# PSUM tiles as single banks, two VectorE instructions for the gating layer's normalised v, and another issue order, in a two-layer diffusion backbone

## The chip, the cores and the metric

The kernel runs on one core of a Trainium2 chip. The metric is the device time of one execution in microseconds (us); where several runs are shown it is their median. The core's engines are TensorE (PE in the profile; PEld is its weight loading), VectorE (DVE), ScalarE (ACT), GpSimd (POOL) and SyncE (SP), which here only issues DMAs.

## The reference

512 latent tokens of width 1024 pass through two layers, with 256 context tokens beside them in the first. Each layer is a token mixer and a SwiGLU feed-forward network (FFN); each of the four sub-layers has an RMS norm before and after it and takes shift, scale and gate rows from the conditioning (adaLN). The first mixer is windowed grouped-query attention, the second a gated MLP whose v half is normalised over its width and mixed over the 128 tokens of a chunk:

```
def layernorm(x, g, b):
    mu = jnp.mean(xf, axis=-1, keepdims=True)
    var = jnp.mean(jnp.square(xf - mu), axis=-1, keepdims=True)
    y = (xf - mu) * lax.rsqrt(var + LN_EPS)
    return (y * g + b)

def chunk_gmlp(h, w_in, b_in, ln_g, ln_b, w_s, b_s, w_o):
    z = jax.nn.gelu(h @ w_in + b_in, approximate=False)
    u, v = jnp.split(z, 2, axis=-1)
    v = layernorm(v, ln_g, ln_b).reshape(bsz, n // CHUNK, CHUNK, B_GROUPS, B_GROUP_W)
    mixed = jnp.einsum('gpq,bnqgc->bnpgc', w_s, v) + b_s.T[None, None, :, :, None]
    return (u * mixed.reshape(bsz, n, B_WIDTH)) @ w_o
```

The FFN is `(silu(h @ w_a) * (h @ w_b)) @ w_out` with a hidden width of 2816. All of it is in float32.

## The kernel before

Every product of matrices is computed as three matmuls in fp32r: each operand is split into a high part, which ACT writes (`w_hi`, `v_hi`, the high half of `H`), and a low part, the rest, which DVE mostly writes (`w_lo`, `v_lo`). hi x hi, hi x lo and lo x hi are added up in PSUM. The 512 tokens lie in four tiles `t` of 128. The stages, by the start of the span: the first norms, keys and queries, attention (to about 240 us), attention's output projection (`WO0`, to 300), FFN0's input half (to 500) and output half (to 625), the gating layer's v and u (to 705), its mixes and its output (`GO`, to 795), FFN1 (to the end).

PSUM has eight banks of 512 float32 for each partition. Outside attention the kernel takes its PSUM tiles from `slot`, which gives tiles of 1024, two banks, of which four exist. Most uses need one bank: `u_part` and `y` write the two halves apart, `mixed`, `head` and `ada_ps` use one half and leave the other. From FFN1's products on, `one_banked` changes to a pool of eight tiles of one bank each.

The FFN's input half forms each block of hidden columns from seven products of quarters, after Strassen (`product`, tile `f`, L1416). A block `n` has three chains in PSUM: 0 takes products 1, 6, 7 and 4, chain 1 takes 5 and 3, chain 2 takes 2. `keep` (ACT, tile `fc`, L1423) copies a chain out between two products. Before the change, in FFN0, chains 0 and 1 of a block lie in one tile, one bank each (`chain`). The output half works the same way on its first columns (`product7`, L1599, tiles `y`, with the adds of L1616 on the results), and plainly on the rest (`plain7`, L1630; its steps are `work_9_t` and `work_10_t` for two units of weights and tile `t`).

At the end of each sub-layer a tile `t` runs through a `Chain`: `square_y` (ACT) and `gain_y` (DVE, L1116) read y from PSUM, then come the power for `ry` on POOL, `add_x` (L1120), `square_x`, the power for `rx`, `gain_x` on POOL (L1132), `shift_x` (L1136), `turn` (PE transposes into `hT`, L1143), and `turned_hi` and `turned_lo`, which write the next `H`. The projection adds an earlier part of y in `merge` (L1104).

In the gating layer tile `t` of v passes a `VChain`: `add` (L1808), `gelu`, `mean`, `var`, `rstd`, `norm` (L1826), `gain` (L1830), `bias` on POOL (L1833), then `v_hi` on ACT and `v_lo` on DVE. The mixes (`mixed`, eight groups of twelve matmuls of 128 columns, L264 to L266) need all four tiles. Beside all this, the rows of adaLN are formed from streamed weights (`add_chunk`, DVE L374, into `acc`; `total`, PE, into `ada_ps`).

The order on each engine is fixed in the program. Steps are entered by `at(time, step)`; a table of names, ORDER, ranks them, and `run_plan` issues them by rank. Each engine executes its own instructions in the order in which they were issued.

Of the kernel before, what the change touches and what calls it, by code (L numbers as in the profile page):

```python
# [157 lines left out]
f0sum_low_S2 f0head_3_2 f0sum_low_S1 f0sum_high_S3 f0part_low_2_1 f0sum_low_S4 f0part_low_2_3 f0sum_low_S3 whigh_43_0  # L158
work_9_0 work_10_0 wlow_43_0 c0square_y#2 whigh_43_1 c0gain_y#2 wfetch_44 work_9_1 c0rstd_y#2 c0add_x#2 work_9_2
# [5 lines left out]
c2shift_x_0#2 c3rstd_y#2 <lambda>_0_0 <lambda>_3_2 <lambda>_0_1 c2shift_x_1#2 c1turned_lo_0#2 c2turn_0#2 c2turn_1#2  # L165
c3add_x#2 whigh_45_1 c1turned_lo_1#2 c3gain_x#2 c2turned_hi_0#2 m2fetch_chunk_0 m2fetch_chunk_1 c3square_x#2
c2turned_hi_1#2 <lambda>_1_0 <lambda>_1_1 c3rstd_x#2 c3shift_x_0#2 c3turn_0#2 c3shift_x_1#2 c2turned_lo_1#2 c3turn_1#2
c2turned_lo_0#2 wlow_45_1 c3turned_hi_1#2 c3turned_hi_0#2 <lambda>_2_0 c3turned_lo_0#2 m2fetch_chunk_2 <lambda>_3_0
<lambda>_2_1 wlow_45_0 <lambda>_3_1 c3turned_lo_1#2 wfetch_46 wfetch_47 m2start#2 lend_u0 v_part_0_(2,) row_in_0
whigh_46_0 row_in_2 whigh_46_1 wlow_46_0 whigh_47_0 row_in_1 wfetch_48 wlow_46_1 m2add_chunk_0 whigh_47_1 bias_in  # L170
v_part_0_(3,) wlow_47_0 m2add_chunk_1 m2fetch_chunk_3 v_part_3_(2,) v_part_1_(2,) v0add m2add_chunk_2 m2fetch_chunk_4
v0gelu m2fetch_chunk_5 v0mean wlow_47_1 ws_in m2add_chunk_3 v0var v0rstd v_part_1_(3,) m2add_chunk_4 m2fetch_chunk_6
v0norm m2add_chunk_5 m2fetch_chunk_7 v_part_2_(2,) v0gain whigh_48_0 whigh_48_1 v1add m2add_chunk_6 u_part_0_0 v1gelu
v0bias v1mean m2add_chunk_7 wlow_48_1 m2fetch_gain#2 v_part_3_(3,) wlow_48_0 m2halve_512#2 m4start#2 m4fetch_chunk_0
m2halve_0#2 v1var v_part_2_(3,) ws_high v1rstd wfetch_49 v0hi v1norm m4fetch_chunk_1 ws_low v1gain v0lo v1bias
m2total_0_slot m2done_0#2 v2add m4add_chunk_0 m4fetch_chunk_2 u_part_0_1 m2total_512_slot m2done_512#2 v2gelu v1hi
v1lo whigh_49_0 u_part_1_0 u_part_1_1 v2mean whigh_49_1 gelu_u_0_0 v3add v2var gelu_u_0_1 wlow_49_0 m4add_chunk_1
m4fetch_chunk_3 wfetch_50 v3gelu v2rstd wlow_49_1 m4fetch_chunk_4 v2norm v3mean v2gain m4add_chunk_2 v3var u_part_2_0
m4add_chunk_3 m4fetch_chunk_5 v2bias v3rstd wfetch_51 m4add_chunk_4 m4fetch_chunk_6 u_part_2_1 v3norm whigh_50_0
v3gain m4add_chunk_5 m4fetch_chunk_7 gelu_u_1_0 gelu_u_1_1 v2hi v2lo m4add_chunk_6 v3bias v3hi v3lo m4add_chunk_7  # L180
m4fetch_gain#2 mixed_0 whigh_50_1 mixed_bias_0 mixed_1 mixed_u_0 mixed_bias_1 wlow_50_0 mixed_5 m4halve_0#2 mixed_3
mixed_u_1 mixed_4 gelu_u_2_0 mixed_2 wlow_50_1 whigh_51_0 mixed_bias_3 mixed_u_3 u_part_3_0 m4halve_512#2 whigh_51_1
mixed_6 mixed_bias_2 mixed_u_2 wlow_51_0 m4total_0_slot mixed_bias_4 mixed_u_4 mixed_bias_5 gelu_u_2_1 wlow_51_1
mixed_u_5 u_part_3_1 m4done_0#2 mixed_7 mixed_bias_6 m4total_512_slot m4done_512#2 gelu_u_3_0 gelu_u_3_1 mixed_u_6
mixed_bias_7 mixed_u_7 whigh_55_0 work_2_0#2 work_3_0#2 whigh_55_1 c0square_y#3 work_2_1#2 wlow_55_1 work_3_1#2
wfetch_56 whigh_56_0 wlow_55_0 whigh_56_1 work_2_2#2 c1square_y#3 c0rstd_y#3 c0gain_y#3 c0add_x#3 m3total_0_slot
m3total_512_slot c0gain_x#3 c0square_x#3 m3done_0#2 work_3_2#2 wlow_56_0 c0rstd_x#3 m3done_512#2 c2square_y#3
c1gain_y#3 c1rstd_y#3 c0shift_x_1#3 c0shift_x_0#3 c1add_x#3 c0turn_0#3 c1gain_x#3 c2gain_y#3 c0turn_1#3 c1square_x#3
c1rstd_x#3 c2rstd_y#3 wfetch_57 c0turned_hi_0#3 work_2_3#2 c1shift_x_0#3 c0turned_hi_1#3 c2add_x#3 c2gain_x#3
work_3_3#2 c1shift_x_1#3 c1turn_0#3 c1turn_1#3 c0turned_lo_0#3 c3square_y#3 c0turned_lo_1#3 c3rstd_y#3 c3gain_y#3  # L190
c2square_x#3 f1head_0_0 c1turned_hi_0#3 c2rstd_x#3 c1turned_hi_1#3 wlow_56_1 f1part_high_2_0 f1first_half_1 c3add_x#3
f1first_half_0 c2shift_x_0#3 f1part_high_2_2 c3square_x#3 c3gain_x#3 c1turned_lo_0#3 f1head_0_1 c3rstd_x#3 f1head_0_2
c2turn_0#3 c1turned_lo_1#3 c2shift_x_1#3 f1diff_2_1 f1first_half_1#2 f1head_1_0 c3shift_x_0#3 f1first_half_0#2
f1diff_2_3 c2turn_1#3 f1head_1_1 c2turned_hi_1#3 c2turned_hi_0#3 c3shift_x_1#3 c3turn_0#3 c3turn_1#3 c3turned_hi_0#3
f1diff_2_2 c3turned_hi_1#3 f1sum_a_S3 f1part_high_2_1 c2turned_lo_0#3 f1sum_a_S2 c2turned_lo_1#3 f1part_low_2_0
f1sum_a_S3#2 f1sum_a_S1 c3turned_lo_0#3 f1head_1_2 f1sum_a_S2#2 f1sum_a_S4 f1sum_a_S1#2 f1head_2_0 f1head_2_1
f1sum_a_S4#2 f1sum_high_S2 f1diff_2_4 c3turned_lo_1#3 f1part_high_2_3 f1head_2_2 f1sum_high_S4 f1part_low_2_1
f1head_3_0 f1sum_low_S4 f1part_low_2_2 f1head_3_1 f1sum_high_S3 wfetch_58 f1sum_high_S1 f1head_3_2 f1sum_low_S1
f1sum_low_S2 f1part_low_2_3 f1sum_low_S3
# [4 lines left out]
def backbone_kernel(ctx: ExitStack, tc: tile.TileContext, a, out):  # L204
# [144 lines left out]
    class Ada:  # L349
# [37 lines left out]
        def total(self, c, bank):  # L387
            st = self.stages.pop(c)
            self.ps[c] = ps = bank("ada_ps")[:, 0:512]
            for z in range(2):  # L390
                nc.tensor.matmul(ps, ones, st[:, z * 512:(z + 1) * 512], start=z == 0, stop=z == 1)
# [688 lines left out]
    def slot(name):  # L1080
        return psM_p.tile([P, D], F32, name=name, tag="b2", bufs=4)
# [9 lines left out]
    class Chain:  # L1091


        def __init__(self, t, ps, G, nxt, part):
            self.t, self.all_ps, self.G, self.nxt, self.ms, self.part = t, ps, G, nxt, [], part

        def y(self, c0, c1):
            if self.part is not None:
                return self.part[:, c0:c1]
            ps = self.all_ps[self.t]  # L1100
            return ps[c0 // 512] if isinstance(ps, tuple) else ps[:, c0:c1]
# [11 lines left out]
        def gain_y(self, c0=0, c1=D):  # L1113
            if c0 == 0:
                self.tmp = big("tmp")
            nc.vector.tensor_tensor(out=self.tmp[:, c0:c1], in0=self.y(c0, c1), in1=self.G[:, c0:c1], op=ALU.mult)  # L1116
# [22 lines left out]
        def turn(self, z):  # L1139
            if z == 0:  # L1140
                self.pt = slot("hT")
            for k in range(4 * z, 4 * z + 4):
                nc.tensor.transpose(self.pt[:, k * P:(k + 1) * P], self.tmp[:, D + k * P:D + (k + 1) * P], ident)  # L1143

        def parts(self, z):
            H, c = self.nxt[2], slice(self.t * P, (self.t + 1) * P)
            return (H[:, 4 * z:4 * z + 4, c], H[:, KC + 4 * z:KC + 4 * z + 4, c],
                    self.pt[:, z * 512:(z + 1) * 512].rearrange("p (k s) -> p k s", k=4))
# [11 lines left out]
    def down(u0, nu, lhs, G_of, nxt_of, head, lend=None, part={}, first=None, also=None, seven=None, bg=None, bg_steps=0):  # L1160
# [4 lines left out]
        ps, sts, left = seven.whole if seven else {}, {}, bg_steps  # L1165
# [7 lines left out]
        def work(v, t):  # L1173
# [5 lines left out]
            if v == v0:  # L1179
                ps[t] = slot(f"y{t}")  # L1180
# [65 lines left out]
    class FFN:  # L1246
        def __init__(self, layer):
            self.layer, self.u0, self.head_ps, self.slot, self.bank = layer, F1[layer], {}, slot, slot
# [26 lines left out]
        def head(self, t, n):  # L1275
# [8 lines left out]
            for k in range(4 * n, 4 * n + 4):  # L1284
                hi, lo = (w[:, (k % 2) * 512:(k % 2 + 1) * 512] for w in parts[(k % 4) // 2])
                mm3(self.head_ps[t][:, 0:512], H[:, k, c], H[:, KC + k, c], hi, lo, k == 0, k == KC - 1)

        def head_gated(self, t):
            pv = self.head_ps[t][:, 0:512].rearrange("p (n z s) -> p n z s", n=2, z=2)
# [8 lines left out]
        def head_turn(self, t, s):  # L1298
            pt = self.slot("fat")
# [12 lines left out]
        def quarters(self):  # L1312
            self.A, self.raw_at, self.T, self.X, self.ps, self.pair, self.c, self.g = {}, {}, {}, {}, {}, {}, {}, {}
# [8 lines left out]
        def first_half(self, q, c):  # L1322

            name = ("S1", "S4")[q]
            if c.t == 0:
                self.sums[name] = self.sum_tile(stage32)
            nc.scalar.copy(out=self.sums[name][:, :, c.t * P:(c.t + 1) * P],
                           in_=c.pt[:, q * 512:(q + 1) * 512].rearrange("p (k s) -> p k s", k=4))
# [4 lines left out]
        def sum_a(self, name, c):  # L1333
# [5 lines left out]
            a21, a22 = (c.pt[:, z * 512:(z + 1) * 512].rearrange("p (k s) -> p k s", k=4) for z in range(2))  # L1339
# [131 lines left out]
        def one_banked(self):  # L1471

            psM.__exit__(None, None, None)
            self.psE = pool("psE", space=PSUM)
            pe = self.psE.__enter__()
            self.bank = self.slot = lambda name: pe.tile([P, 512], F32, name=name, tag="bk", bufs=8)

        def rest(self, nxt_of, head, rows=(), **kw):
# [30 lines left out]
            for i in range(KC * len(sums)):  # L1509
# [8 lines left out]
                if k == KC - 1:  # L1518
                    at(b + .1, e.fetch_gain)
                    for z in range(2):  # L1520
                        at(b + T * (.25 + .85 * z), e.halve, z * 512, nc.vector)
                        at(b + T * (.25 + .85 * z) + 3.7, e.total, z * 512, self.bank)
# [515 lines left out]
```

## Time and profile before

| | |
|---|---|
| three runs | 1132.28, 1132.56, 1134.19 us |
| profiled execution | 1132.03 us, span 1130.3 us |
| mean granted PE clock | 0.991 of full |
| busy | PE 98%, DVE 85%, ACT 54%, POOL 23% |
| read from HBM | 171.71 MB, 154 GB/s over the span |

In the rows of groups, the columns are line, engine, operation, out<-in, shapes, count, then busy time and the mean of one in ns, then the idle time of the engine before them and what ended it. In the rows of a timeline, the first number is the start, the second the duration, and the bracket the idle time before with its releaser. A row of waits gives the total, the count and the longest. A row of windows gives, for each engine, busy time and count of instructions, and near its end the granted clock. Matmuls are pipelined, so a row's duration is longer than the step to the next.

### The profile page before, as it was taken

The numbers are of one execution on the slowest core, as the hardware profiler recorded it, in microseconds if no ns is written. First come the engines' busy times: TensorE is split into PE (matmuls) and PEld (weight loads), VectorE is DVE, ScalarE is ACT, GpSimd is POOL, SyncE is SP. The second block draws the span as 40 slices with busy tenths as digits, with TensorE's granted clock in tenths as the row PEclk, the third lists the DMA queues.
The fourth block names the chain that finished last, engine by engine and source line by source line (L and its number), as shares of the span: only waits on it lengthen the run. The fifth ranks groups of instructions, "written<-read, shape, count | busy, mean of one in ns | idle before, by whom it ended". The sixth has DMA issues, their size and how long they took to land.

```text
span 1130.3 us, 17929 instructions
## 1 busy us (share of the span) xinstructions
PE 1107.2 (98%) x7038; PEld 973.2 (86%) x7038; DVE 959.9 (85%) x1398; ACT 614.0 (54%) x1049; POOL 265.6 (23%) x245
## 2 busy tenths in 40 slices
PE   8999999999999999999999999999999999999997
PEld 5789877768899999998887788888899999998876
DVE  6788988959999999988977879867988888879985
ACT  6357768666544555455564534246555555546552
POOL 2347575514600000002312314005400000002400
PEclk9999999999999999999999999799999999999999
DMA  9742332233255554469935376443134333459921
GB/s 370 283 138 93 114 112 76 76 138 106 93 166 174 183 170 163 153 223 278 218 63 168 109 255 233 138 161 108 41 131 149 132 111 133 150 177 322 176 35 75
DMA packets 47577, 174.97 MB, mean 155 GB/s; under 512 B 4602, under 2 KB 8954, under 8 KB 36356
## 3 DMA queue, kind: packets, MB, share of 16 engines
q1 hardware_dynamic: 40580, 161.24, 40.7%
q0 software_dynamic: 6912, 12.59, 6.6%
q8 instruction: 55, 0.90, 0.3%
q14 instruction: 30, 0.25, 0.1%
HBM read 171.71 MB, written 2.10 MB: 154 GB/s over the span
## 4 chain that ended last, share of the span: by engine, by line
PE 84%; DVE 9%; ACT 3%; issue 3%; DMA 1%; POOL 0%; SPq 0%; DVEq 0%; POOLq 0%; ACTq 0%
PE f L1416 32%; PE y L1599 13%; PE y L272 7%; PE y L1630 5%; PE v L272 4%; PE s_ps L882 3%; PE o_ps L935 2%; PE pT_ps L915 2%; DVE w_lo L220 2%; PE q_ps L264 1%; PE q_ps L266 1%; PE q_ps L265 1%; PE kv L264 1%; DVE a_sum L1342 1%; PE kv L265 1%
## 5 line engine op out<-in xcount | busy, mean ns | idle before, releaser
L1416 PE MATMUL f<-H,w_hi 128*128 128x256 f32 x960 | 178.1, 283 | 0.0
L1587 POOL DMA_DIRECT2D t<-in_w x48 | 42.3, 933 | 492.6 <-PE y L1630 216.1
L1416 PEld LDWEIGHTS f<-H,w_hi 128*128 128x128 f32 x960 | 150.0, 192 | 0.5
L1416 PE MATMUL f<-H,w_lo 128*128 128x256 f32 x480 | 135.7, 283 | 0.0
L1599 PE MATMUL y<-w_hi,s 128*128 128x512 f32 x448 | 120.8, 390 | 0.8 <-DVE y L1616 0.8
L1416 PE MATMUL f<-S,w_hi 128*128 128x256 f32 x640 | 120.0, 285 | 0.0
L217 ACT CAST w_hi<-w_raw 128x1024 fp32r<-128x1024 f32 x90 | 94.3, 1051 | 39.4 <-PE y L1599 12.2
L217 ACT CAST w_hi<-T 128x1024 fp32r<-128x1024 f32 x80 | 83.7, 1048 | 57.0 <-PE f L1416 27.1
L1423 ACT COPY fc<-f 128x256 f32<-128x256 f32 x120 | 44.6, 373 | 119.0 <-PE f L1416 116.8
L220 DVE TENSOR_TENSOR w_lo<-w_raw,w_hi 128x1024 fp32r<-128x1024 f32 (+1 forms) x77 | 92.8, 1208 | 9.0 <-ACT w_hi L217 9.0
L1599 PEld LDWEIGHTS y<-w_hi,s 128*128 128x128 f32 x448 | 83.9, 188 | 19.0 <-DVE y L1616 1.3
L1416 PEld LDWEIGHTS f<-S,w_hi 128*128 128x128 f32 x640 | 99.5, 192 | 0.4
L220 DVE TENSOR_TENSOR w_lo<-T,w_hi 128x1024 fp32r<-128x1024 f32 x80 | 97.2, 1215 | 0.0
L1416 PEld LDWEIGHTS f<-H,w_lo 128*128 128x128 f32 x480 | 92.1, 192 | 0.0
L1416 PE MATMUL f<-S,w_lo 128*128 128x256 f32 x320 | 90.6, 283 | 0.5 <-DVE w_lo L220 0.5
L374 DVE SCALAR_TENSOR_TENSOR acc<-ada_k,sc,acc 128x1024 f32<-128x1024 f32 x56 | 75.4, 1346 | 5.7 <-DMA ada_k<-in_ada 3.6
L1599 PE MATMUL y<-w_lo,s 128*128 128x512 f32 x224 | 69.1, 390 | 0.6 <-DVE w_lo L220 0.6
L909 POOL TENSOR_SCALAR p<-p,st 128x512 f32<-128x512 f32 (+1 forms) x64 | 55.8, 885 | 43.3 <-DVE st L905 25.1
L1416 PE MATMUL f<-H,x 128*128 128x256 f32 x480 | 64.2, 283 | 0.0
L1416 PEld LDWEIGHTS f<-S,w_lo 128*128 128x128 f32 x320 | 61.3, 192 | 0.7 <-DVE w_lo L220 0.7
L888 DVE CUSTOM_DVE_ANT_0 s_ps<-s_ps,mask,nsink 128x512 f32<-128x512 f32 (+1 forms) x64 | 51.8, 816 | 11.7 <-PE s_ps L882 9.5
L272 PE MATMUL y<-w_hi,st 128*128 128x512 f32 x224 | 61.2, 391 | 0.3 <-ACT uT L1858 0.3
(263 smaller groups left out, 2891.0 us busy)
## 6 DMA issues: line engine op xcount, KB each, us to landing
w_raw<-in_w SPq DMA_DIRECT2D x67, 1024.0 KB, 5.1
ada_k<-in_ada SPq DMA_DIRECT2D x56, 512.0 KB, 5.8
ada_raw<-in_ada SPq DMA_DIRECT2D x12, 1024.0 KB, 5.1
w<-in_w SPq DMA_DIRECT2D x12, 1024.0 KB, 8.8
t<-in_w POOLq DMA_DIRECT2D x48, 256.0 KB, 5.9
ada<-in_ada SPq DMA_DIRECT2D x8, 1024.0 KB, 12.2
t<-in_w SPq DMA_DIRECT2D x8, 1024.0 KB
w_raw<-in_w SPq DMA_DIRECT2D x10, 512.0 KB
```

Source lines behind the costliest of these rows:

```text
L217: nc.scalar.copy(out=hi, in_=src)
L220: (eng or nc.vector).tensor_tensor(out=lo, in0=src, in1=hi.bitcast(F32), op=ALU.subtract)
L272: nc.tensor.matmul(dst, l, w[:, n * 512:(n + 1) * 512], start=first and i == 0, stop=last and i == 2)
L374: nc.vector.scalar_tensor_tensor(out=self.acc, in0=self.raws.pop(k), scalar=sc[:, k:k + 1], in1=self.acc, op0=ALU.mult, op1=ALU.add)
L882: nc.tensor.matmul(dst, self.qT[:, j, :], keys, start=i == 0, stop=i == 1)
L888: nc.vector.tensor_tensor_reduce(out=s, in0=s, in1=self.msk, scale=-1.0, scalar=nsink[:, h:h + 1], op0=ALU.add, op1=ALU.min, accum_out=sel ...
L909: nc.gpsimd.tensor_scalar(out=p, in0=p, scalar1=self.st[:, 12 + j:13 + j], scalar2=1.0, op0=ALU.mult, op1=ALU.mult)
L1416: nc.tensor.matmul(dst, l[:, w], r[:, k, :], start=first and k == 0 and j == 0, stop=k == 3 and j == 2, skip_group_check=True)
L1423: nc.scalar.copy(out=self.c[n][:, i * 256:(i + 1) * 256], in_=self.ps[n, 1 if i == 1 else 0])
L1587: nc.gpsimd.dma_start(out=self.tt[:, p * D + 512 * i:p * D + 512 * (i + 1)], in_=a["w"][F2[self.layer] + 1 + 2 * p + i][:, c:c + 512], acc ...
L1599: nc.tensor.matmul(self.bank7(i, j), st[:, c:c + P], w[:, z * 512:(z + 1) * 512], start=i == 1 and p == 0 and l == 0 and z == 0, stop=p == ...
L1630: nc.tensor.matmul(self.y[t][n], st[:, x + t * P:x + (t + 1) * P], parts[h][w][:, n * 512:(n + 1) * 512], start=v == 0 and h == 0 and i == ...
```

## The change

1. `slot` gives one bank, eight of which exist; `slots` gives a pair of such tiles for y and v. Tiles `f`, `u`, `mix`, `hT`, `fat`, `fa` and `ada_ps` become single banks, and chains 0 and 1 of a block are two tiles. `one_banked` goes. An instruction that read 1024 columns of a two-bank tile becomes two of 512: `merge`, `square_y`, `gain_y` and VChain's `add`.
2. VChain's `norm` goes. `gain` forms (w - mu) x gain and `bias` forms that x r + bias, each one scalar_tensor_tensor on DVE; `bias` leaves POOL. `gain` needs no longer the power `rv`, `bias` does.
3. ORDER is another one from FFN0's output half on.

```
-        return psM_p.tile([P, D], F32, name=name, tag="b2", bufs=4)
+        return psM_p.tile([P, 512], F32, name=name, tag="bk", bufs=8)
+
+    def slots(name):
+        return tuple(slot(f"{name}{n}") for n in range(2))
+
+    def halves(c0, c1):
+        return [(c, min(c + 512, c1)) for c in range(c0, c1, 512)]
...
         def merge(self):
-            nc.vector.tensor_tensor(out=self.part, in0=self.all_ps[self.t], in1=self.part, op=ALU.add)
+            for c0, c1 in halves(0, D):
+                p = self.part[:, c0:c1]
+                nc.vector.tensor_tensor(out=p, in0=self.all_ps[self.t][c0 // 512], in1=p, op=ALU.add)
...
         def square_y(self, c0=0, c1=D):
-            self.ms.append(mean_square(self.y(c0, c1), "msy"))
+            for c in [(c0, c1)] if self.part is not None else halves(c0, c1):
+                self.ms.append(mean_square(self.y(*c), "msy"))
...
-            nc.vector.tensor_tensor(out=self.tmp[:, c0:c1], in0=self.y(c0, c1), in1=self.G[:, c0:c1], op=ALU.mult)
+            for a0, a1 in [(c0, c1)] if self.part is not None else halves(c0, c1):
+                nc.vector.tensor_tensor(out=self.tmp[:, a0:a1], in0=self.y(a0, a1), in1=self.G[:, a0:a1], op=ALU.mult)
...
         def chain(self, n, ch):
 
-            if ch == 1 and self.bank is slot:
-                return self.pair[n][:, 512:768]
-            self.pair[n] = ps = self.bank(f"f{ch}")
-            return ps[:, 0:256]
+            return slot(f"f{ch}")[:, 0:256]
...
-        def one_banked(self):
-
-            psM.__exit__(None, None, None)
-            self.psE = pool("psE", space=PSUM)
-            pe = self.psE.__enter__()
-            self.bank = self.slot = lambda name: pe.tile([P, 512], F32, name=name, tag="bk", bufs=8)
...
-            nc.vector.tensor_tensor(out=self.v, in0=v_ps[self.t], in1=rows[0], op=ALU.add)
+            for n, (c0, c1) in enumerate(halves(0, D)):
+                nc.vector.tensor_tensor(out=self.v[:, c0:c1], in0=v_ps[self.t][n], in1=rows[0][:, c0:c1], op=ALU.add)
...
-        def norm(self):
-            nc.vector.tensor_scalar(out=self.v, in0=self.w, scalar1=self.mu[:, 0:1], scalar2=self.r,
-                                    op0=ALU.subtract, op1=ALU.mult)
-
         def gain(self):
-            nc.vector.tensor_tensor(out=self.v, in0=self.v, in1=rows[1], op=ALU.mult)
+            nc.vector.scalar_tensor_tensor(out=self.v, in0=self.w, scalar=self.mu[:, 0:1], in1=rows[1],
+                                           op0=ALU.subtract, op1=ALU.mult)
 
         def bias(self):
-            nc.gpsimd.tensor_tensor(out=self.v, in0=self.v, in1=rows[2], op=ALU.add)
+            nc.vector.scalar_tensor_tensor(out=self.v, in0=self.v, scalar=self.r, in1=rows[2],
+                                           op0=ALU.mult, op1=ALU.add)
...
-f0sum_low_S2 f0head_3_2 f0sum_low_S1 f0sum_high_S3 f0part_low_2_1 f0sum_low_S4 f0part_low_2_3 f0sum_low_S3 whigh_43_0
-work_9_0 work_10_0 wlow_43_0 c0square_y#2 whigh_43_1 c0gain_y#2 wfetch_44 work_9_1 c0rstd_y#2 c0add_x#2 work_9_2
+f0sum_low_S2 f0head_3_2 f0sum_low_S1 f0sum_high_S3 f0part_low_2_1 f0sum_low_S4 f0part_low_2_3 f0sum_low_S3 work_9_1
+whigh_43_0 work_9_0 work_10_0 wlow_43_0 c0square_y#2 whigh_43_1 c0gain_y#2 wfetch_44 c0rstd_y#2 c0add_x#2 work_9_2
```

What the table does on PE near the end of FFN0's output half, where the last of `product7` (L1599) meets `plain7` (L1630 before, L1626 after). The number in a tile's name after `y` is its `t`; after the change a second digit is the bank. Before:

```order
L1599 MATMUL y3_5860<-w_lo_6469,s7_6464 128x512 x2
L1599 MATMUL y3_5860<-w_hi_6468,s7_6464 128x512 x2
L1630 MATMUL y0_5893<-w_lo_6496,st_6510 128x512 x2
L1630 MATMUL y0_5893<-w_hi_6495,st_6510 128x512 x2
L1630 MATMUL y0_5893<-w_hi_6514,st_6529 128x512 x2
L1630 MATMUL y0_5893<-w_lo_6515,st_6529 128x512 x2
L1630 MATMUL y0_5893<-w_hi_6514,st_6529 128x512 x2
L1630 MATMUL y0_5893<-w_hi_6533,st_6536 128x512 x2
L1630 MATMUL y0_5893<-w_lo_6534,st_6536 128x512 x2
L1630 MATMUL y0_5893<-w_hi_6533,st_6536 128x512 x2
```

After, at the same place:

```order
L1599 MATMUL y30_5899<-w_lo_6511,s7_6506 128x512 x2
L1599 MATMUL y30_5899<-w_hi_6510,s7_6506 128x512 x2
L1626 MATMUL y10_5958<-w_lo_6538,st_6552 128x512
L1626 MATMUL y11_5959<-w_lo_6538,st_6552 128x512
L1626 MATMUL y10_5958<-w_hi_6537,st_6552 128x512
L1626 MATMUL y11_5959<-w_hi_6537,st_6552 128x512
L1626 MATMUL y00_5933<-w_hi_6526,st_6529 128x512
L1626 MATMUL y01_5934<-w_hi_6526,st_6529 128x512
L1626 MATMUL y00_5933<-w_lo_6527,st_6529 128x512
L1626 MATMUL y01_5934<-w_lo_6527,st_6529 128x512
```

Tile 1 has taken the place of tile 0 around the last products, and tile 0's unit 9, twelve matmuls, now stands behind them, ahead of its unit 10. From tile 0's last matmul to the first `hT` PE has 60 matmuls before and 48 after.

On DVE, the end of v's chains in the gating layer. Before, from the last `norm` on:

```order
L1826 TENSOR_SCALAR vtmp<-vtmp,mu,rv 128x1024
L1830 TENSOR_TENSOR vtmp<-vtmp,row_6898 128x1024
L374 SCALAR_TENSOR_TENSOR acc<-ada_k,sc,acc 128x1024
L220 TENSOR_TENSOR v_lo<-vtmp,v_hi 128x1024
L374 SCALAR_TENSOR_TENSOR acc<-ada_k,sc,acc 128x1024
L220 TENSOR_TENSOR v_lo<-vtmp,v_hi 128x1024
L374 SCALAR_TENSOR_TENSOR acc<-ada_k,sc,acc 128x1024
```

After, from the last `gain` (L1823) on; L1827 is `bias`:

```order
L1823 SCALAR_TENSOR_TENSOR vtmp<-vtmp,mu,row_6964 128x1024
L374 SCALAR_TENSOR_TENSOR acc<-ada_k,sc,acc 128x1024
L220 TENSOR_TENSOR v_lo<-vtmp,v_hi 128x1024
L374 SCALAR_TENSOR_TENSOR acc<-ada_k,sc,acc 128x1024
L1827 SCALAR_TENSOR_TENSOR vtmp<-vtmp,rv,row_6965 128x1024
L220 TENSOR_TENSOR v_lo<-vtmp,v_hi 128x1024
L374 SCALAR_TENSOR_TENSOR acc<-ada_k,sc,acc 128x1024
```

The bias of the last tile now stands on DVE between the last two `v_lo`, with the high part of that tile, on ACT, still to come after it; POOL's part is gone. On PE the order of the mixes moves as well: before, 72 mixes stand between the first three pairs of u and the next, and 12 after that; now 84 stand in one run.

More of the change, by code (lines that the diff above doesn't have):

```diff
@@ L1139, in turn @@
         def turn(self, z):
[L1140 to L1143, printed above, removed]
+            self.pt[z] = slot("hT")
+            for k in range(4):
+                c = D + z * 512 + k * P
+                nc.tensor.transpose(self.pt[z][:, k * P:(k + 1) * P], self.tmp[:, c:c + P], ident)
         def parts(self, z):
@@ L1892, in backbone_kernel @@
             at(5.45 * t + 2.72 * (u - 2), v_part, t, (u,))
[L1893 to L1894 removed]
+        for b, f in ((0, c.add), (1.2, c.gelu), (2.5, c.mean), (2.8, c.var), (4.1, c.rstd), (3.3, c.gain),
+                     (5, c.bias), (6.4, c.hi), (7.5, c.lo)):
             at(5.45 * (t + 1) + b, f)
```

122 lines of the change are left out of this document (57 added, 65 removed).

## The prediction

> **What bounds the kernel now.** I read the page first, for the busy times, the granted clock and the chain that ended last.
>
> ```profile
> PE 1107.2 (98%) x7038; PEld 973.2 (86%) x7038; DVE 959.9 (85%) x1398; ACT 614.0 (54%) x1049; POOL 265.6 (23%) x245
> PEclk9999999999999999999999999799999999999999
> PE 84%; DVE 9%; ACT 3%; issue 3%; DMA 1%; POOL 0%; SPq 0%; DVEq 0%; POOLq 0%; ACTq 0%
> ```
>
> PE is busy 98% of the span. The change takes no matmul away, so it can gain only what PE loses: the 2% in which it waits, and the slice with the 7, in which PE was busy at a lower clock. VectorE (85%) is second, so work that is given to it is not free wherever PE already waits for it. Next I read the waits of PE, taking those in stages that the change touches.
>
> ```profile
> PE f L1416 <- ACT fc L1423: 1.9, 3, 1.0
> PE mix L266 <- DVE v_lo L220: 1.5, 1, 1.5
> PE y L1630 <- DVE w_lo L220: 1.4, 1, 1.4
> PE hT L1143 <- DVE tmp L1136: 1.3, 2, 0.8
> PE y L1599 <- DVE y L1616: 0.8, 1, 0.8
> PE fa L266 <- DVE H L220: 0.7, 1, 0.7
> PE ada_ps L391 <- ACT row L396: 0.7, 1, 0.7
> ```
>
> Together 8.3 us are within reach, plus what the lower clock costs. Everything below is a change against the profiled execution, 1132.03 us (span 1130.3 and 1.7 around it), which is 0.5 below the median of the runs, 1132.56.
>
> **FFN0's products.** The timeline of ACT and PE at the longest of the three waits for `fc`:
>
> ```profile
> 431.42 1.05 ACT L217 CAST w_hi<-T 128x1024 fp32r<-128x1024 f32 x1 [1.68 <-DVE T L1373]
> 431.75 0.40 PE L1416 MATMUL f<-H,w_hi 128*128 128x256 f32 x2
> 432.00 0.28 PE L1416 MATMUL f<-H,w_lo 128*128 128x256 f32 x1
> 432.89 0.36 ACT L1423 COPY fc<-f 128x256 f32<-128x256 f32 x1
> 433.31 0.51 PE L1416 MATMUL f<-s,w_hi 128*128 128x256 f32 x2 [1.03 <-ACT fc L1423]
> ```
>
> The product that starts at 433.31 writes chain 1. The copy that it waited for reads chain 0, which lies in the other bank of the same tile; ACT reached it late, behind a cast that was itself waiting for `T`. With a tile for each bank this product needs only the copy of its own chain, which stands earlier on ACT. The next product of chain 0, twelve matmuls later, still needs the late copy: twelve at 0.125 us (two from 431.75 to 432.00) are 1.5 us, more than the 1.0 waited. So I take the three waits as gone: 1.9, and 0.5 for the pipeline's restarts, **-2.4**. Bounds: -2.4, and 0 if ACT's lateness simply reaches the next product.
>
> **Split instructions.** What one full-width instruction and two halves cost, and what the change of the gating layer exchanges, by the groups:
>
> ```profile
> L1116 DVE TENSOR_TENSOR tmp<-y,row 128x1024 f32<-128x1024 f32 x10 | 12.2, 1218 | 4.6 <-ACT junk L235 4.6
> L1116 DVE TENSOR_TENSOR tmp<-y,row 128x512 f32<-128x512 f32 x8 | 5.5, 689 | 5.3 <-ACT junk L235 5.2
> L235 ACT ACTIVATE junk<-y 128x1024 bf16<-128x1024 f32 x10 | 10.2, 1024 | 16.0 <-PE y L1630 8.1 <-PE y L272 7.9
> L235 ACT ACTIVATE junk<-y 128x512 bf16<-128x512 f32 x8 | 4.8, 597 | 15.4 <-PE y L1630 15.3
> L235 ACT ACTIVATION_READ_ACCUMULATOR junk<-y 128x1 f32 x18 | 3.5, 195 | 0.0
> L1808 DVE TENSOR_TENSOR vtmp<-v,brow 128x1024 f32<-128x1024 f32 x4 | 4.9, 1216 | 5.0 <-PE v L272 5.0
> L1826 DVE TENSOR_SCALAR vtmp<-vtmp,mu,rv 128x1024 f32<-128x1024 f32 x4 | 3.2, 812 | 2.0 <-POOL rv L245 2.0
> L1120 DVE SCALAR_TENSOR_TENSOR x<-tmp,ry,x 128x1024 f32<-128x1024 f32 x15 | 19.2, 1280 | 3.3 <-POOL ry L245 3.1
> L1830 DVE TENSOR_TENSOR vtmp<-vtmp,row 128x1024 f32<-128x1024 f32 x4 | 4.9, 1220 | 0.0
> L1833 POOL TENSOR_TENSOR vtmp<-vtmp,row 128x1024 f32<-128x1024 f32 x4 | 12.3, 3066 | 11.2 <-DVE vtmp L1830 11.2
> ```
>
> A split gain costs DVE 2 x 0.689 - 1.218 = 0.16 us more, a split square costs ACT 2 x (0.597 + 0.195) - (1.024 + 0.195) = 0.37 more, so a tile's way from y to the next H grows by 0.53. Ten tiles are concerned: the end of attention's projection, of FFN0 and of the gating layer. While PE has matmuls of other tiles to do, this is hidden. Without that cover it costs 0.5 a tile. At the projection's end I charge one tile and its merge, **+0.6** (0 to 2.1).
>
> **FFN0's output half.** The timeline of PE and ACT, with two rows that give the pace of 512-wide matmuls:
>
> ```profile
> 594.05 0.73 PE L1599 MATMUL y<-w_hi,s 128*128 128x512 f32 x2 [0.83 <-DVE y L1616]
> 605.34 0.74 PE L1630 MATMUL y<-w_lo,st 128*128 128x512 f32 x2 [1.44 <-DVE w_lo L220]
> 606.58 1.02 ACT L235 ACTIVATE junk<-y 128x1024 bf16<-128x1024 f32 x1 [1.40 <-PE y L1630]
> 616.84 1.07 PE L1630 MATMUL y<-w_hi,st 128*128 128x512 f32 x4
> 617.75 0.62 PE L1630 MATMUL y<-w_lo,st 128*128 128x512 f32 x2
> 620.02 1.04 PE L1143 MATMUL hT<-ident,tmp 128*128 128x128 f32 x8
> ```
>
> The wait at 594.05 is again for the other bank of a tile, and goes. The one at 605.34 is a weight whose low part is late. `work_9_1`, twelve matmuls of tile 1, now stand ahead of it, which are 12 x 0.2275 = 2.7 us of cover (0.91 us for four), so it goes too: 0.8 + 1.4 and two restarts, 2.6. But tile 0 is complete no earlier, since those twelve now precede it: 606.5 less 2.6 plus 2.7. From its first square to the first `hT` are 13.4 us before (606.58 to 620.02), under 60 matmuls (13.7 us); now 48 stand there, 10.9 us. PE would come 2.5 too early by the old way of tile 0. That way gets shorter, because before its shifts stood behind tile 1's gain and add, and tile 1 is now complete 24 matmuls after tile 0 instead of 36, so they are done by then; it gets longer by 0.5. I take half of the 2.6: **-1.2** (-2.2 to +0.5).
>
> **The gating layer.** The timeline around the last v tile:
>
> ```profile
> 701.60 3.31 POOL L1833 TENSOR_TENSOR vtmp<-vtmp,row 128x1024 f32<-128x1024 f32 x1 [2.25 <-DVE vtmp L1830]
> 702.56 3.42 DVE L220 TENSOR_TENSOR v_lo<-vtmp,v_hi 128x1024 fp32r<-128x1024 f32 x1
> 707.11 1.21 DVE L220 TENSOR_TENSOR v_lo<-vtmp,v_hi 128x1024 fp32r<-128x1024 f32 x1
> 708.38 0.33 PE L266 MATMUL mix<-ws_hi,v_lo 128*128 128x128 f32 x1 [1.50 <-DVE v_lo L220]
> ```
>
> The same DVE instruction takes 3.42 beside POOL's bias and 1.21 alone. Per tile DVE loses norm and gain, 0.81 + 1.22, and gets two scalar_tensor_tensor, which at the 1.28 of the chain's add into x make +0.5, with +0.16 for the split add. It gains some 2 us for each bias that no longer runs beside it, and the chain loses 3.07 of POOL for about 1.3 of DVE. The last v_lo should be over 2 us earlier against PE, the wait was 1.5: **-1.3**, with 0.2 kept for a chunk of weights that lands late (0 to -1.7).
>
> **The gating layer's output.** Eight banks instead of four pairs free the `ada_ps` wait of 0.7. The waits for `hT` and `H` behind it (0.8 and 0.7) may take it back, with 0.5 a tile from the splits: **-0.4** (-1.4 to +2.1).
>
> **The clock.** The windows view, cut at the borders at which the granted clock changes, 3.41 us apart:
>
> ```profile
> 78.63:82.04 3.41, 1.83 (x7) 1.16 (x7) 1.95 (x4) 3.38 (x5) 3.29 (x4) 1.00 0.00 0
> 430.20:433.61 3.41, 2.38 (x20) 2.17 (x19) 2.32 (x4) 2.19 (x4) 0.00 (x0) 1.00 0.47 133
> 706.68:710.10 3.42, 1.92 (x17) 1.78 (x17) 3.42 (x4) 0.80 (x3) 0.95 (x1) 1.00 0.03 6
> 713.51:716.92 3.41, 3.41 (x17) 3.41 (x18) 3.41 (x5) 1.26 (x3) 0.00 (x0) 0.50 0.23 38
> 720.34:723.75 3.41, 3.41 (x9) 2.64 (x9) 3.38 (x4) 0.00 (x0) 0.00 (x0) 0.50 0.54 197
> ```
>
> From 710.10 to 723.75, four such windows, the clock is 0.50. Half of that, 6.8 us, is the most that full clock can return; as 128-wide mixes run a little better than half, I take 6.5. The window ahead of it holds the mix wait: 17 matmuls of 128 columns, 2,176, where a full stream of 512-wide ones passes 15 x 512 = 7,680, a share of 0.28. The window at 78.63, also followed by half clock, has 7 of at most 512, under 0.47. The one at 430.20 has about 18 of 256, 0.60, and kept its clock. A window of mixes alone, without a wait, would have about twice the 16 that 713.51 to 716.92 shows at half clock, a share of 0.5: between the two cases. At half clock such mixes did not bring the clock back; 512-wide ones did, at 723.75. I find it a little likelier that mixes alone are too few. Then the throttle starts inside the run of 84 mixes, one window earlier or later by where they fall, and lasts four windows, or three: **-0.8** (0 to -3.3).
>
> The Trainium skill, "TensorE: Matmul & The Clock Gate", Part 1, has the rate drop after an idle window of about 3.4 us and rise after a busy one. By that rule no window of the new run would be idle and the clock would stay, as in the first rival. The trace agrees on the window (3.41) and differs on idleness: PE was busy 1.92 of 3.42 us ahead of a drop.
>
> Sum: -2.4 + 0.6 - 1.2 - 1.3 - 0.4 - 0.8 = -5.5, so 1126.5 us.
>
> **The rivals.** *The clock stays up.* Without the 1.5 us hole the windows hold enough, all 6.5 come back in place of 0.8: 1132.0 - 4.7 - 6.5 = 1120.8. For it: both drops had a hole in the window ahead. Against: mixes alone at half clock never woke it.
>
> *The chains end later than PE.* Every tile of the three down stages is 0.53 longer, and FFN0's end has 48 matmuls of cover instead of 60. If tile 0's way stays 13.4 + 0.5 against 10.9, PE waits 3.0 there and 0.5 at each of three more tiles, less the 1.3 of `hT` waits before: +3.2, against the 2.6 removed, +0.6. The other two stages give their upper ends, +2.1 each, since PE already waits there. With the products' waits only moved (0) and the mixes' wait unchanged behind the later H, the sum is +4.8, or 1136.8; with the products' 2.4 gained it is 1134.4, which I take. It decides once PE's waits for `hT`, `H` and `tmp` pass some 6 us (2.0 before). Against: POOL is freed and tile 1 comes earlier.
>
> *Nothing to be had.* The waits named are those inferred last; behind each another stands (the low part of a weight, ACT's lateness) and half of each returns, with the clock as before: about -2, 1130.
>
> **How the numbers follow.** A measurement of this kernel can tell about 0.2%, 2.3 us, from no change. Clock drops as before, with the waits gone: 0.46, 1126.5 (own range 1123.5 to 1129). Clock stays: 0.37, 1120.8 (1118.5 to 1123). Chains late: 0.09, 1134.4. Little: 0.08, 1130. The range takes the first two with their bounds, 1118 to 1130, and leaves out most of the last two. Faster than 1129.8: nearly all of the first two and half of the fourth, 0.86; the same 0.06; slower 0.08.
>
> **What would show it.** Right: no wait of `f` for `fc`, none of `y` for a `y` add, none at the mixes, v_lo at 1.2 us each; the clock row shows a 0.50 stretch in the mixes again. Wrong: a full clock row there (then 1121), hT waits over 3 us at FFN0's end, or DVE waits of `f` after the projection over 2 us.

## The result and the profile after

The kernel after takes 1116.32 us in the median of its runs (1115.61 to 1116.72), the kernel before on the same chip 1133.38 (1132.28 to 1134.25): a ratio of 0.9849, 95% interval 0.9832 to 0.9866. That is 17 us faster, 10 below the forecast of 1126.5 and below the range's lower end of 1118. The two profiled executions differ by 15.3 us; the stages below account for those.

The page of the kernel after, the rows that answer to those of before (busy times, granted clock, chain):

```profile
PE 1095.5 (98%) x7038; PEld 964.8 (87%) x7038; DVE 952.4 (85%) x1414; ACT 618.7 (55%) x1069; POOL 257.8 (23%) x241
PEclk9999999999999999999999999999999999999999
PE 89%; DVE 5%; ACT 2%; issue 1%; POOL 1%; DMA 1%; SPq 0%; DVEq 0%; POOLq 0%; ACTq 0%
```

The 7 in the row of the clock is gone. PE's busy time fell by 11.7 us with the same 7038 matmuls. At most 8.5 of that is the clock: ahead of its end the kernel before ran 17.1 us at half clock, 13.65 in the mixes and 3.41 at 82 us, where the stage was none the longer for it. Pauses too short to count as idle are another part (below, at FFN0's input half). The chain runs over PE for 89% instead of 84%. The waits of PE in the stages that the change touches are these:

```profile
PE hT L1153 <- DVE tmp L1146: 1.4, 3, 0.7
PE y L272 <- DVE oT L946: 0.8, 1, 0.8
PE y L1599 <- DVE w_lo L220: 0.6, 1, 0.6
PE f L1423 <- DVE w_lo L220: 0.5, 1, 0.5
```

No `f` waits for `fc`, no `y` for a y add, no mix for `v_lo`, no `ada_ps`, no `fa`. The wait for `oT`, at the start of the projection, is new. To see where the time went, the span is cut at the first PE instruction of each stage (start times of the traces, in us). The last columns belong to experiments 1 to 4 below: banks alone, v chain alone, banks with order, banks with v chain.

| stage | before | after | 1 banks | 2 v chain | 3 banks, order | 4 banks, v chain |
|---|---|---|---|---|---|---|
| to the first y of the projection | 241.9 | 243.5 | 241.7 | 242.0 | 241.6 | 241.5 |
| to FFN0's first f | 59.2 | 60.1 | 60.9 | 59.3 | 61.0 | 61.0 |
| to FFN0's first y | 208.0 | 204.0 | 204.0 | 207.9 | 204.0 | 204.0 |
| to the first hT | 110.9 | 107.7 | 109.5 | 110.9 | 107.7 | 109.5 |
| to the first v | 5.3 | 6.0 | 5.3 | 5.3 | 6.0 | 5.3 |
| v and u, to the first mix | 80.2 | 79.9 | 79.9 | 80.2 | 79.9 | 79.9 |
| mixes and last u, to the next y | 31.2 | 22.6 | 30.9 | 28.8 | 30.9 | 32.1 |
| to FFN1's first f | 73.8 | 71.7 | 73.0 | 73.8 | 71.7 | 73.0 |
| to the last matmul | 312.7 | 312.6 | 312.7 | 312.7 | 312.5 | 312.7 |

Between before and after: +1.6, +0.9, -4.0, -3.2, +0.7, -0.3, -8.6, -2.1, -0.1, together -15.1 of the 15.3 between the two spans. The mixes' stage alone gave more than half. FFN1 had single banks already, and did not change. The +1.6 at the start is a wait of 1.8 us of `kv` in this execution (experiment 9 has it too); the change touches nothing there, and a second profile of the same kernel (experiment 10) has 241.7.

### The profile page after: what moved, and what is told of

It is laid out like the page before. It is cut to its first block, busy times and chain, and to the rows that moved or that the text cites. A ratio compares the mean times of both kernels' runs of the same rounds, so it can differ in the third digit from the quotient of the medians.

```text
span 1115.0 us, 17943 instructions
## 1 busy us (share of the span) xinstructions
PE 1095.5 (98%) x7038; PEld 964.8 (87%) x7038; DVE 952.4 (85%) x1414; ACT 618.7 (55%) x1069; POOL 257.8 (23%) x241
## 4 chain that ended last, share of the span: by engine, by line
PE 89%; DVE 5%; ACT 2%; issue 1%; POOL 1%; DMA 1%; SPq 0%; DVEq 0%; POOLq 0%; ACTq 0%
PE f L1423 36%; PE y L1599 13%; PE y L272 7%; PE y L1626 4%; PE v L272 4%; PE s_ps L882 3%; PE o_ps L935 2%; PE pT_ps L915 2%; PE u L1843 1%; PE u L1845 1%; PE u L1844 1%; PE q_ps L264 1%; PE q_ps L266 1%; PE q_ps L265 1%; PE kv L264 1%
## 5 line engine op out<-in xcount | busy, mean ns | idle before, releaser
L1599 PE MATMUL y<-w_hi,s 128*128 128x512 f32 x448 | 120.1, 389 | 0.0
L1599 PEld LDWEIGHTS y<-w_hi,s 128*128 128x128 f32 x448 | 84.1, 188 | 17.5
L374 DVE SCALAR_TENSOR_TENSOR acc<-ada_k,sc,acc 128x1024 f32<-128x1024 f32 x56 | 71.6, 1278 | 9.5 <-DMA ada_k<-in_ada 7.3
L1599 PE MATMUL y<-w_lo,s 128*128 128x512 f32 x224 | 69.1, 390 | 0.6 <-DVE w_lo L220 0.6
```

The lines of the kernel that those rows point to most:

```text
L374: nc.vector.scalar_tensor_tensor(out=self.acc, in0=self.raws.pop(k), scalar=sc[:, k:k + 1], in1=self.acc, op0=ALU.mult, op1=ALU.add)
L1599: nc.tensor.matmul(self.bank7(i, j), st[:, c:c + P], w[:, z * 512:(z + 1) * 512], start=i == 1 and p == 0 and l == 0 and z == 0, stop=p == ...
```

## The experiments

**1. Single banks alone.** The kernel after with the old ORDER and the old VChain but for its split `add`:

```
 kernel after:
-ORDER of the change
+ORDER of before
-        def gain(self):  (w - mu) * row1 on DVE
-        def bias(self):  v * r + row2 on DVE
+        def norm(self), gain(self), bias(self) of before, bias on POOL
```

> Single banks alone: the kernel after with the old VChain (bias on POOL) and the old ORDER. Theory (the waits in FFN0 came from tiles shared by two banks, the hole and the clock in the mixes from the v chain): FFN0's input half, from its first product to the first y, falls from 212.3 to about 208.3 us, its output half loses the 1.0 us at the y adds, the mixes' stage (first mix to first y of the gating output) stays near 31.2 us with the clock at 0.50 in four windows. About 1133.4 - 5 = 1128.5. Rival 1 (the new order of issue removed those waits): 1133, with the three waits of f for fc still there. Rival 2 (the clock dropped for want of banks): the mixes' stage is 22.6 us, 1120.

1125.46 us against 1132.05 for before on the same chip, ratio 0.9938 (0.9915 to 0.9961). That is 3 us less than expected. FFN0's input half took 204.0, which is 4.0 less, as expected (the expectation counts the stage from an earlier start), and its output half lost 1.4. In the profiled execution the mixes kept a wait of 1.6 us and the half clock, for 13.65 us as before, and their stage 30.9. The theory holds there and both rivals fall. Three of the ten runs, with 1119.5 to 1121.7 us at mean clocks of 0.998 and 0.999, seem to have kept the clock in spite of the wait. The banks alone give 4.0 in FFN0's input half, 1.4 in its output half and 0.8 in the gating layer's output, and cost 1.7 at the projection.

**2. The two VectorE instructions alone.** The kernel before with this:

```
-        def norm(self): ...
-        gain:  v * row1 on DVE;  bias:  v + row2 on POOL
+        gain:  (w - mu) * row1 on DVE;  bias:  v * r + row2 on DVE
```

> The two VectorE instructions for normalised v alone: the kernel before with the new gain and bias, nothing else. Theory: v_lo of the last tile comes before the mix that needs it, the hole of 1.5 us is gone or under 0.5, the clock stays at 1.00 through the mixes, whose stage takes 22.6 instead of 31.2 us: 1133.4 - 8.6 = 1125. Rival 1 (the last v_lo also needs the new order or the banks, since it was only 0.3 us ahead of need): a hole of about 1 us stays and the clock with it, 1131 to 1133. Rival 2 (bias on DVE delays other work): slower than 1133.4.

1130.03 against 1132.05, 0.9985 (0.9972 to 0.9998): 2 us, not 8.6. The hole shrank to 0.4, but PE's longest wait is a new one. Its waits, and the timeline of PE and DVE around the new one:

```profile
PE u L1847 <- DVE m L1866: 2.8, 1, 2.8
PE mix L266 <- DVE v_lo L220: 0.4, 1, 0.4
```

```profile
716.36 0.68 DVE L1866 TENSOR_TENSOR m<-mix,bs 128x512 f32<-128x512 f32 x1
717.09 0.79 PE L1847 MATMUL u<-H,w_hi 128*128 128x512 f32 x1 [2.76 <-DVE m L1866]
```

The u behind the mixes needs a PSUM tile, and the four tiles of two banks are all held by mixes that VectorE has not read. At full clock PE arrives there earlier than VectorE has read them; before, at half clock, no such wait stands in the profile. The clock fell during the wait, for two windows (6.83 us at 0.50 from 715.1). The theory was right on the cause of the first hole and wrong on the price: none of the rivals named this wait. With single banks and the same v chain (experiment 4) u waits for no tile.

**3. Banks and order, old v chain.** The kernel after with the VChain of before (the same edit as in 1, ORDER left as after).

> The kernel after with the old VChain: norm, gain, and bias on POOL; banks and order as after. Theory: a wait of the mixes for v_lo over 1 us returns, and with it four windows at half clock: 1116.3 + 8 = about 1124 to 1125, all other stages as after. Rival (the banks and the order of the mixes were what kept the clock): the wait is under 0.5, the clock full, 1116 to 1118.

1125.00 against 1132.05, 0.9936 (0.9916 to 0.9955). The wait for `v_lo` is 1.7, the clock 0.50 for 13.65 us, the mixes' stage 30.9, all other stages within 0.9 of after but the start, which lacks the `kv` wait of that execution. As the theory has it: here the v chain is worth some 9 us.

**4. Banks and v chain, old order.** The kernel after with the ORDER of before.

> The kernel after with the old ORDER; banks and v chain as after. Theory: FFN0's input half and the mixes are as after (208.3 and 22.6 us); only the output half of FFN0 keeps the late weight at its plain part (1.6 us) and is about 111 instead of 109.4 us; the gating output a little longer: 1118 to 1119. Rival (the order is what keeps v_lo ahead of the mixes): the hole and half clock return, 1124 or more.

1122.21 against 1132.05, 0.9904 (0.9887 to 0.9921). The waits of the mixes:

```profile
PE mix L266 <- DVE v_lo L220: 0.8, 1, 0.8
PE mix L264 <- ACT v_hi L217: 0.2, 1, 0.2
```

The rival holds for the profiled run: the last `v_lo` comes 0.8 too late under the old order, and the clock is at 0.50 for 17.07 us, five windows. In the other three runs, by their mean clocks of 0.998 and 0.999 and 1120.3 to 1123.2 us, it mostly stayed up. The order is also worth 1.1 from FFN0's first y to the first v and 1.3 at the gating layer's output. So in the profiled executions the mixes' 8.6 us take all three parts: with single banks the v chain shortens the hole from 1.6 to 0.8, the order takes the rest, and the banks keep the next u from waiting for a tile. In most runs with the old order the clock held without the last part.

**5. A shared tile again.** The kernel after, but:

```
         def chain(self, n, ch):
-            return slot(f"f{ch}")[:, 0:256]
+            if self.layer == 0 and ch == 1:
+                return self.pair[n][:, 256:512]
+            ps = slot(f"f{ch}")
+            if ch == 0:
+                self.pair[n] = ps
+            return ps[:, 0:256]
```

The two chains now lie in one bank as well, which before they did not, and FFN0's sums here are not the reference's; instructions and sizes are unchanged.

> The kernel after, but in FFN0 chain 1 of a block lies in the upper half of chain 0's tile (one bank here), so that the two share a tile again. Theory (FFN0's input half lost 4.0 us to waits for the other chain's copy): the three waits of f for fc return, about 1.9 us, and the pauses of some 0.09 us, one for each block (17 of them), 1.5: the input half is 207 to 208 instead of 204.0 us and the time 1116.3 + 3 to 4 = 1120. Rival (it was the number of buffers, eight instead of four): 204.0 and 1116.

1121.09 against 1131.69, 0.9911 (0.9874 to 0.9948), 5 above after. The input half took 208.8, a little more than expected. The waits for the other chain's copy are back, with eight tiles all the same:

```profile
PE f L1428 <- ACT fc L1435: 2.2, 4, 1.0
```

So it is the sharing and not the number of tiles. That it is the tile, and not a common bank, is seen from before against experiment 1. The window from 420 to 440 us, with the longest of the waits, for before, after and this kernel, in this order (time, PE busy with its count of matmuls):

```profile
420.00:440.00 20.00, 18.96 (x156) 18.66 (x155) 18.14 (x25) 9.74 (x16) 0.00 (x0) 1.00 0.50 161
```

```profile
420.00:440.00 20.00, 20.00 (x167) 19.92 (x166) 18.90 (x26) 11.70 (x20) 0.00 (x0) 1.00 0.53 171
```

```profile
420.00:440.00 20.00, 18.96 (x156) 18.64 (x155) 17.75 (x26) 11.10 (x20) 0.00 (x0) 1.00 0.53 174
```

**6 and 7. A made hole in the mixes.** The kernel after with one and with two needless adds:

```
         def lo(self):
+            for _ in range(1 if self.t == 3 else 0):     # 2 in the second
+                nc.vector.tensor_tensor(out=self.w, in0=self.v, in1=rows[2], op=ALU.add)
             low(vlo[:, self.t, :], vhi[:, self.t, :], self.v)
```

> The kernel after with one needless VectorE add of 1.2 us ahead of the last v_lo, so that the mixes wait about 0.8 us. Theory (the clock drops after a window of 3.41 us that holds under about 0.4 of a stream's columns; mixes alone hold 0.48): the share of the window with the hole is 0.37 to 0.45, by where its borders fall, so this is the edge: 1117.1 without a drop, up to 1124 with one, differing from run to run. Rival 1 (any wait in the mixes drops it): 1124 in every run. Rival 2 (only an idle window does): 1117.1 in every run.

> The same with two such adds, a wait of about 1.9 us in the mixes. Theory: a window with the whole hole holds 0.21 of a stream's columns, the clock drops for four windows, 1116.3 + 1.9 + 6.5 = about 1124.5; where a border cuts the hole in two, less. Rival (only a wait near a whole window drops it): 1118.2, full clock.

With one add 1115.69 against 1131.69, 0.9860 (0.9819 to 0.9902), the same as after: it made no hole, since it ran in the 1.1 us in which VectorE waits for ACT's `v_hi`. I had not counted that wait. One of its four runs took 1119.93, at a mean clock of 0.996. With two adds 1124.27, 0.9937 (0.9916 to 0.9958), near the 1124.5 expected, but in the profiled execution not for the reason expected: the mixes waited 0.7 and the clock stayed up through them, while two later waits at the gating output came in:

```profile
PE y L272 <- DVE row L398: 3.1, 1, 3.1
PE y L272 <- DVE m L1864: 2.4, 1, 2.4
```

VectorE, one add later than in after, misses further on, and there the clock drops too (6.83 us from 735.0). The stage to FFN1's first f is 80.5 instead of 71.7. Six of the nine runs had lower mean clocks, 0.990 to 0.993 against 0.996 in the profiled one, so they spent longer at half clock; where is not known, and there the expected drop in the mixes may have come. What was meant to measure the clock measured VectorE's slack: beyond the 1.1 us of waiting for `v_hi`, it has less than one add of 1.2 us.

**8. Free tiles for u by pairing mixes.** The kernel of experiment 2 with two mixes in each two-bank tile:

```
-        mix[g] = ps = slot("mix")
+        n = len(mix)
+        i, z = (n % 3, n // 3) if n < 6 else (3, n - 6)
+        mix_of[i] = mix_of.get(i) or slot("mix")
+        mix[g] = ps = mix_of[i][:, z * 512:(z + 1) * 512]
```

> The kernel before with the new gain and bias, and with the mixes two to a two-bank tile, so that the u after them finds a free tile. Theory (with the new v chain alone, u waited 2.8 us for a tile that a mix held until VectorE read it, and that wait dropped the clock): the wait of u for m is gone, the clock stays at 1.00, the mixes' stage is 22.6 to 23.2 instead of 28.8 us, 1130.0 - 5.8 = about 1124.5. Rival (u waits for VectorE's lateness in another way, or the clock drops all the same): 1128 to 1130.

1133.73 against 1131.69, 1.0018 (0.9998 to 1.0037). The wait of u is gone as expected, the time is not:

```profile
PE ada_ps L391 <- DVE m L1869: 4.3, 1, 4.3
```

The next taker of a tile, `ada_ps`, waits 4.3 us instead, and the clock drops there. The stage is 31.1. FFN1's first f waits 1.9 as well, with one more window at half clock. The theory's 1124.5 falls, and the rival's 1128 to 1130 was too low: with tiles of two banks the wait moved to whoever asked next.

**9. gain_x of FFN0's end on VectorE.** An attempt to beat the kernel after, whose tile 0 is the limit at the first hT:

```
-            nc.gpsimd.tensor_tensor(out=self.tmp[:, D:], in0=x[:, self.t, :], in1=self.nxt[0], op=ALU.mult)
+            self.mul.tensor_tensor(out=self.tmp[:, D:], in0=x[:, self.t, :], in1=self.nxt[0], op=ALU.mult)
...
+        for c in ch:
+            c.mul = nc.vector if seven else nc.gpsimd
```

In ORDER, each gain_x of that stage stands behind its add_x, and the shifts of tiles 0 and 1 stand together.

> The kernel after with gain_x of FFN0's end on VectorE instead of POOL, each directly behind its add_x, and the two shifts of tiles 0 and 1 together. Theory (after the change PE waits 1.0 us for hT there because tile 0's way is the limit, and POOL's 2.4 to 2.9 us gain, which can begin only when the add is done, is its longest step): the waits for hT at 616 and 620 us go, the stage from the first y to the first v is shorter by 0.7 to 1.3 us, 1115.0 to 1115.6 where the kernel after has 1116.3. Rival (VectorE's adds of other tiles queue behind the four gains, 1.2 us each): no gain, or 0.5 slower.

1127.05 against 1132.26, 0.9944 (0.9930 to 0.9957): 11 us slower than after. The gain costs VectorE 1.23 us a tile, 4.9 in all, and it has no room for them:

```profile
PE y L272 <- DVE m L1864: 2.6, 2, 2.1
PE v L272 <- DVE H L220: 1.5, 1, 1.5
PE u L1847 <- DVE w_lo L220: 1.3, 1, 1.3
```

The wait of 0.75 for tile 0's hT did go, and reappears as waits of a later hT (0.9), of v, u and the gating output; up to the first v the stage gained 0.2 at most. Against experiment 10 the profiled execution, the slowest of its five, lost 4.9 us at its start, which the edit doesn't touch (`kv` waited 1.8 there, and the clock fell twice for 3.41 us). It then lost 1.3 in v, 1.6 in the mixes and 5.4 at the gating layer's output: these waits stand there, and at the output another 3.41 us at half clock. The run with the least time still took 1125.17.

**10. The kernel after again.**

> The kernel after once more, for comparison on the same chip: 1116.3, clock full through the mixes in every run, since mixes alone hold 0.48 of a stream's columns in a window; the rival (the clock drop depends on where the windows' borders fall even without a wait) expects some runs at 1120 to 1122.

1115.75 against 1132.26, 0.9863 (0.9842 to 0.9883), with the mixes at 22.6 and full clock in the profile. One of its four runs took 1120.99 at a lower mean clock (0.996 against 0.998 to 0.999), as the rival has it and not the theory: a drop still occurs at times; where, is not known. One run of the first comparison had 0.996 too, and took no longer for it (1116.29). None of the kernels tried here was clearly faster than the kernel after.

## Why the prediction was wrong

The direction was right, and so were the waits that were to go. The main step, on the clock, was wrong, and three terms were too small. With the clock's term put right the sum would have been 1120.8, within the range; the three terms took the time below it.

- **The clock: the step that failed.** The prediction took it as a little likelier that "mixes alone are too few", and gave the clock -0.8 where -6.5 was to be had. They were enough here: the mixes of the kernel after ran at full clock throughout. The windows view of the kernel after, a whole window of mixes, and below it those of experiments 1, 3 and 4 that come ahead of a drop:

```profile
702.80:706.22 3.42, 3.42 (x33) 3.42 (x33) 3.28 (x5) 2.98 (x5) 0.00 (x0) 1.00 0.53 152
```

```profile
702.03:705.44 3.41, 1.85 (x17) 1.71 (x16) 3.41 (x4) 0.79 (x2) 0.95 (x1) 1.00 0.04 11
```

```profile
702.17:705.58 3.41, 2.49 (x22) 2.50 (x23) 3.35 (x4) 1.32 (x3) 0.74 (x1) 1.00 0.15 17
```

```profile
700.61:704.03 3.42, 2.42 (x17) 2.02 (x16) 2.31 (x3) 1.99 (x2) 0.60 (x1) 1.00 0.01 4
```

  The counts in brackets take in matmuls that reach over a border. 33 mixes of 128 columns kept the clock, 17 and 22 lost it, and so did 13 with a few u ahead of them. Eight profiles have such a window, filled with mixes alone at full clock, and each kept it. The prediction set its 0.5 for such a window between 0.47 (lost) and 0.60 (kept). But 0.47 was only an upper bound: the seven matmuls at 78.63 were four of 512 columns and three of 256, a share of 0.37, so 0.5 lay nearer to the window that kept it. The prediction's first rival, 1120.8, was the right case, though the time lies outside the rival's own range too (1118.5 to 1123). Hole and clock were priced together at -2.1, or -7.8 in the rival; the stage gave -8.6.
- **FFN0's input half, -2.4: right cause, too small.** It gave -4.0. The three waits, with their restarts, come to 2.7. Beside them stand 17 pauses of about 0.09 us, one a block at a product of chain 0, which no row of waits shows: 1.5 together. They are gone with the tiles apart. A pair of such matmuls takes 0.49 us from start to end before (first line) and 0.40 after:

```profile
418.99 0.49 PE L1416 MATMUL f<-S,w_hi 128*128 128x256 f32 x2
```

```profile
419.39 0.40 PE L1423 MATMUL f<-S,w_hi 128*128 128x256 f32 x2
```

- **The projection's end, +0.6: the size by luck.** +0.9 to +1.8 in the kernels with single banks, but 0.76 of it is at the projection's start: the second matmul of its first y, which writes the second bank, waits for `oT`, which VectorE forms from attention's `o_ps`.

```profile
244.64 0.47 PE L272 MATMUL y<-w_hi,st 128*128 128x512 f32 x1 [0.76 <-DVE oT L946]
```

  All nine profiles with single banks have this wait (0.7 to 0.8), and none of the three with tiles of two. That this bank was one of `o_ps`'s is likely but not shown. Waits of the projection's `hT`, which the splits would bring, are 0.3 in experiments 1, 3 and 5 and none in after.
- **FFN0's output half, -1.2: too small.** -2.5 up to the first v. Experiment 1 gives 1.4 of it to the banks, and 1 against 3 the other 1.1 to the order. Half of the 2.6 was taken, nearly all of it came. The prediction read the 13.4 us from the first square to the first `hT` as the time that tile 0 needs. But no wait stands ahead of that `hT`, at 620.02: this line of before has the first half of tile 0 ready at 617.92.

```profile
617.18 0.74 DVE L1136 SCALAR_TENSOR_TENSOR tmp<-tmp,rx,row 128x512 f32<-128x512 f32 x1
```

  The 13.4 was PE's cover. What tile 0 needs up to its second half went from 13.7 us (606.58 to 620.31) to 12.2 (604.38 to 616.58), and PE waits 0.75 for that half. hT waits 1.4 in all against 1.3 before.
- **The gating layer's v.** `norm` and `gain` became two instructions of 1.28, and `v_lo` no longer slows down. The groups of the kernel after:

```profile
L1827 DVE SCALAR_TENSOR_TENSOR vtmp<-vtmp,rv,row 128x1024 f32<-128x1024 f32 x4 | 5.1, 1278 | 0.0
L220 DVE TENSOR_TENSOR v_lo<-vtmp,v_hi 128x1024 fp32r<-128x1024 f32 x4 | 4.9, 1221 | 1.5 <-ACT v_hi L217 1.5
```

  The price of 1.28 and the step from 3.42 to 1.21 held (one of the four `v_lo` had taken 3.42; beside the other three additions of POOL stood an `add_chunk`). "Over 2 us earlier against PE" was a little too much: the last v_lo ended 1.4 too late before, and now ends at 702.0, 0.3 ahead of its mix, which makes 1.8.

```profile
697.19 1.28 DVE L374 SCALAR_TENSOR_TENSOR acc<-ada_k,sc,acc 128x1024 f32<-128x1024 f32 x1 [1.72 <-DMA ada_k<-in_ada]
700.79 1.22 DVE L220 TENSOR_TENSOR v_lo<-vtmp,v_hi 128x1024 fp32r<-128x1024 f32 x1 [1.12 <-ACT v_hi L217]
702.34 0.28 PE L266 MATMUL mix<-ws_hi,v_lo 128*128 128x128 f32 x1
```

  For the chunk of weights that lands late, for which 0.2 was kept, VectorE waited 1.72 us here; the mixes did not wait.
- **The gating layer's output, -0.4: too small.** -2.1, of which 0.8 by the banks and 1.3 by the order (experiments 1 and 3). The waits for `ada_ps` and `fa` both went.
- **Not in the prediction:** the wait for a tile that the v chain alone brings (experiment 2). The text counted the banks as a gain at `ada_ps` and did not ask who would want a tile once the mixes ran at full clock. Since the change brings the banks too, it cost nothing here. It also bears on the 6.5 us that full clock was to return. The kernel before took 1126.7 to 1128.9 us in the 8 of its 47 executions beside the experiments that had a mean clock of 0.997 or 0.998, and 1131.2 to 1138.3 in the others, at 0.988 to 0.993. By these, an estimate, the drop costs that kernel some 4 to 5 us; a wait like that of experiment 2 in its place would fit the difference, but no trace shows one.
- **The rival that ended slower** (chains later than PE) did not occur: PE waits 1.6 us for `hT`'s `tmp` and for `H`, far from the 6 at which it decides.

## What to carry to other kernels

Two results that share a tile are one object to whoever waits for it, even in two banks: a copy of the one holds back the write of the other, and part of the cost, here 1.5 of 4.0 us, stands in no list of waits. When the clock drops behind a wait, price the wait and the clock together and ask what share of a window the work keeps once the wait is gone. And a wait that is removed at half clock moves the point at which the next resource runs out; look for the next taker of a buffer before counting the gain.

## What the runs showed of the hardware

The granted clock changed at borders 3.41 us apart. As a measure of such a window, take the columns of the matmuls that start in it as a share of 7,680, what fifteen matmuls of 512 columns pass in one at full clock. Outside the first 16 us of a span, every window at full clock with a share of 0.35 or less lost the clock at its end (0.25 before and in experiment 1, 0.35 in 2 and 4), and none above 0.47 did: 30 or 31 mixes alone make 0.50 to 0.52. From 0.37 to 0.47 both occur: experiment 3 lost it in the mixes with 0.37 and experiment 9 at 30.2 us with 0.47, while after kept it at 27.0 us with 0.40 and experiment 8 at the first mixes with 0.45. In the first 16 us windows down to 0.18 kept it. So the share goes with the clock in the mixes but is not the whole rule, which stays open. In the mixes' stage the clock did not come back after windows of 16 or 17 mixes at half clock, and did after windows that seven or eight matmuls of 512 columns filled. The same kernel with the same wait did not always lose it: see the mean clocks of the kernel before above. The Trainium skill, "TensorE: Matmul & The Clock Gate", Part 1, lets the rate fall after an idle window; the runs agree on the window's length, and differ in that PE was busy for 1.85 to 2.49 of the 3.41 us in the three windows ahead of a drop that are quoted above.

A VectorE subtraction of two operands in SBUF took 3.42 us beside a GpSimd addition of 3.31 and 1.22 without it. In the kernel before, one VectorE instruction with its tensors in SBUF began during each of the four additions, and each ended 1.08 or 1.09 us after the addition did. An `add` of v, which reads one operand from PSUM, ran inside one of the additions in its usual 1.21. The Trainium skill, "SBUF — State Buffer", section "SBUF: two separate sides", says that the two share a port that one of them holds for a whole instruction while the other is blocked; these numbers agree.
